# An encoder layer on one core: projection steps, scan pieces and denominators change places in the mixers

## The chip, the cores and the metric

The kernel runs on one core of a Trainium2 chip. The metric is the device time of one execution in microseconds (us). TensorE (PE in the profile; PEld is its weight load) multiplies matrices into PSUM, VectorE (DVE), ScalarE (ACT) and GpSimd (POOL) work element by element, and SyncE (SP) issues most of the transfers between memories (DMAs). Each engine works off its own instructions in order and waits for others by semaphores. The shape is fixed: 1024 tokens of width 1024, float32.

## The reference

The layer projects its input, runs two kinds of heads side by side ("mixers"), projects back, and then runs a gated feed-forward part:

```python
u      = x @ w_in                      # rq, rk, rv, rg (4 x 512), aq (512), ak, av (2 x 128)
y_ret  = silu(rg) * GroupNorm(retention_forward + retention_backward)   # 8 heads of 64
y_att  = windowed_gqa(aq, ak, av, sink)                                 # 8 heads, 2 kv heads, window 128
h      = LN1(2**0.25 * x + concat(y_ret, y_att) @ w_out)
f      = (silu(h @ w_gate) * (h @ w_up)) @ w_down + sigmoid(h @ w_pg) * (p @ w_pe)
out    = LN2(2**0.25 * h + f)
```

Retention in one direction works in chunks. Within a chunk it is `(q k^T * decay) v`. Across chunks a state is carried: each chunk makes the product `k^T v`, a scan turns these into states (state * chunk decay + product), and `q * decay` times the state is added. The backward direction does the same from the end. Attention sees, for a block of 128 queries, the blocks before, at and behind it; its scores get a bias by distance, an exponential, and a division by the sum of the exponentials plus that of a sink.

## The kernel before

Every large product is made of three matmuls on numbers split in a high and a low part (`mm3`, L83 to L86), each with 128 x 512 outputs. The whole runs in three parts: first projections, the mixers (until about 378 us), and the rest, which starts with the product by `w_out` (lines L884 to L886).

**Steps of projection as filler.** The remaining input projections stand in a list, `queue` (L286). One entry is one *step*: three matmuls of `mm3` for one block of 128 of the inner dimension. Eight steps fill half a tile and end in an eviction. `take(k)` (L291) issues the next k steps and counts them in `ticks`. Work with a due count (`later`, `side`) is issued as soon as the count of steps reaches it: so a lag is a number of steps. `run(list, total)` (L788) walks a list by hand: each `F` (None) stands for an equal share of `total` steps, everything else is called where it stands. The order of TensorE's instructions is this order exactly (`manual_schedule`, L801). VectorE, ScalarE, GpSimd and SyncE are ordered by a planner, which goes by the order of issue and by when it expects operands; an instruction wrapped in `behind` (L88) is not placed ahead of the last `mm3` issued before it.

**Mixers.** `i = 0` runs attention pair 0 first (L811 to L814), then retention pair 0 (L824). For `i = 1, 2, 3` retention pair i and attention pair i run together in one list with 48 steps (L852); they are called mixers 1, 2 and 3 below. The steps there are projections for pair i + 1, in mixer 3 the gates: gate(0) in steps 1 to 16, each half evicted by L783 to L785 after its eighth step. The last list (L866) has 16 steps.

The parts of a mixer, in the list's names:
- `K(q)`: transposes half of the retention keys; ScalarE evicts them with the decay (L428).
- `C(d)`: products k^T v of direction d (L443), into both banks "t" (forward) or both banks "s" (backward); evicted by VectorE and ScalarE (L450, L452) into `U`, whose buffer is tagged "qq" (forward) or "pt" (backward).
- `S_(d, part)`: the scan of direction d on VectorE in two pieces (L460): part 0 is one wide addition and three small ones, part 1 three small ones, one wide one, and two transfers of the result into `states` (L471).
- `sco(n)`: scores of attention block n (L583, L584), each into a bank "s"; VectorE adds the bias (L585), ScalarE takes the exponential (L588). After blocks 3 and 7 the denominators' reciprocals are made on small tiles (`sums`, L593 to L597).
- `trn(n)`: transposes block n's exponentials (L623) into banks "t"; ScalarE copies them back (L628). At n = 3 and 7 one more transposition takes the reciprocals of four blocks along (L626); they go out to memory and come back as one row for all partitions (`spread`, L601; store L608, fetch L612).
- `val(n)`: values of attention block n (L640), into a bank "o"; after n = 3 and 7 VectorE multiplies by the reciprocals (`times`, L645), LAGV steps later.
- `r.scores`: retention scores (L482) into both banks "s", then VectorE multiplies them by the decay into a tile tagged "pt" (L485).
- `Q(hh)`: VectorE multiplies queries by the decay (L496).
- `r.out`: retention output into both banks "o" (L508, L513); `E(t)` evicts it (L522 to L525).
- `M(t)`: sums of squares by a matmul (L532, L534); then, LAGS steps later each, `spread` to 128 partitions (L539), power on GpSimd (L542), store (L545), fetch as factors (L549), and on VectorE the multiplication `scaled` (L553).

There are two banks of each tag in PSUM, so a matmul that wants a bank "s" waits until the one before last is emptied. In parallel, weights of later products are split and stored to memory in the gaps (`put`, L662 to L665). `first_loads` (L859) loads the first four operands of the product by `w_out`, two into buffers tagged "w", two into buffers tagged "raw"; buffers "raw" are also used by the last split of weights, whose two halves are due at steps 50 and 53 counted from the start of mixer 3.

Of the kernel before, what the change touches and what calls it, by code (L numbers as in the profile page):

```python
# [16 lines left out]
P = 128  # L17
# [5 lines left out]
NPAIR = 4  # L23
# [7 lines left out]
LAGA = (2, 1, 4)  # L31
LAGS = (3, 6, 9, 12, 15)
LAGX = 4
LAGV = 5
NLAG = 7


# [12 lines left out]
def layer(tc, xT, xn, w_first, w_mt, w_rv, w_out, w_pg, w_pe, pT, w_gu, w_dn,  # L50
          consts, dec_b, dec_c, sink, gng, lnp, out):
    nc = tc.nc
    act, dve, pool, pe, sp = nc.scalar, nc.vector, nc.gpsimd, nc.tensor, nc.sync
# [16 lines left out]
    def bank(tag, shape=(P, HF)):  # L70
        tag = ROLE[tag]
        return ps.tile(list(shape), F32, tag=tag, bufs=NB[tag], name=nm("b" + tag))
# [21 lines left out]
    last = {}  # L94
# [62 lines left out]
    with tc.manual_schedule(engines={mybir.EngineType.DVE, mybir.EngineType.SP}):  # L157
        for kt in range(KT):
            r = xraw[kt]
# [44 lines left out]
    ident = cst[:, C_ID:C_ID + P]  # L204
# [67 lines left out]
    for h in range(2):  # L272
        sl = slice(h * HF, (h + 1) * HF)
        b = st[1, h]
        for g in range(2):
            a = slice(64 * g, 64 * g + 64)
# [129 lines left out]
    class Retention:  # L406
# [121 lines left out]
        def norm(self, t):  # L528

            b = self.o[t].rearrange("p n c -> p (n c)")  # L530
            for k in range(2):
                pe.matmul(b[0:NONE], ones, self.sq[t][k], start=k == 0, stop=k == 1)  # L532
            row = bt([2, HF], ("rb", "kv1")[t])
            behind(dve.tensor_scalar(row, b[0:2], 1.0 / 64, EPS, ALU.mult, ALU.add))  # L534
            sm, r, home = bt([P, 2, 8], "sn", 1), bt([P, HF], ("rb", "kv1")[t]), rnd[2 * self.i + t]

            def spread():
                for h in range(2):
                    sp.dma_start(sm[64 * h:64 * h + 64, 0], row[h:h + 1].rearrange("o (q e) -> o q e", e=8))  # L539

            def power():
                behind(pool.tensor_tensor(sm[:, 1], sm[:, 0], cst[:, C_MH:C_MH + 1].to_broadcast([P, 8]), ALU.pow))  # L542

            def store():
                sp.dma_start(home, sm[:, 1])  # L545

            def fetch():
                for h in range(2):
                    sp.dma_start(r[64 * h:64 * h + 64], home[64 * h:64 * h + 64].rearrange("q e -> (q e)").partition_broadcast(64))  # L549

            def scaled():
                y = self.half(t)
                behind(dve.scalar_tensor_tensor(y, y, gn[:, self.i:self.i + 1], r.rearrange("p (n c) -> p n c", c=CH),  # L553
                                                ALU.mult, ALU.mult))

            late = 0 if self.i else LAGX
            later.extend((ticks[0] + at, f) for at, f in zip(LAGS, (spread, power, store, fetch)))
            later.append((ticks[0] + LAGS[4] + late, scaled))

# [3 lines left out]
    class Attention:  # L563
# [53 lines left out]
        def turn(self, n):  # L617
            lo, hi = span(n)
            self.pt[n] = []
            for g in range(2):  # L620
                tb = bank("t", (P, 4, P))
                for kb in range(hi - lo):
                    pe.transpose(tb[:, kb, :], self.sc[n][g][:, kb * P:(kb + 1) * P], ident)  # L623
                last = not g and n % 4 == 3
                if last:
                    pe.transpose(tb[0:8, 3, :], self.st[n // 4][:, 3].rearrange("p j g -> p (j g)"), ident)  # L626
                p_ = self.sc[n][g].rearrange("p (k q) -> p k q", q=P)
                act.activation(p_[:, :hi - lo, :], tb[:, :hi - lo, :], AF.Copy)  # L628
                self.pt[n].append(p_)
                if last:  # L630
                    self.spread(n // 4, tb[0:8, 3, :])

        def values(self, n):
            hh, j = divmod(n, 4)
# [7 lines left out]
            if j == 3:  # L642
# [3 lines left out]

                later.append((ticks[0] + LAGV, times))

# [139 lines left out]
    def run(steps, total):  # L788

        shares = steps.count(None)  # L790
        done = n = 0
        for f in steps:
            if f is None:
                n += 1
                take(total * n // shares - done)
                done = total * n // shares
            else:
                f[0](*f[1:])

    F = None  # L800
    with tc.manual_schedule(engines={mybir.EngineType.PE}):  # L801
        enqueue([mtile(0, ev_av), proj_rv(), *project(1), *project(2), *project(3), gate(0), gate(1), gate(2), gate(3)])

        spare.append(bt([P, S], "aq", 3, F32R))
        twin = lambda t: t.rearrange("p (a b) -> p a b", a=2)
        ops = [twin(spare[1]), a_tile([P, 2, HF], "pro", "A0", F32R)]
        side.extend(presplit_out(0, ops, 17.5, 4))
        side.extend(presplit_out(1, ops, 44, 4, spare[:1]))
        a = Attention(0, ytile(1))
        sco, trn, val = (lambda n: (a.scores, n)), (lambda n: (a.turn, n)), (lambda n: (a.values, n))  # L810
        run([F, F, sco(0), F, sco(1), F], 16)  # L811
        run([F, (av_turn, 0), (av_turn, 1), F, trn(0), sco(2), F, trn(1), sco(3), F, trn(2), F,
             trn(3), F, val(0), val(1), val(2), val(3), sco(4), F, sco(5), F, trn(4), sco(6), F, trn(5), sco(7), F, trn(6), (decay_q, 0),
             F, trn(7), (decay_k, 0, 0), F, val(4), val(5), val(6), val(7), (decay_k, 0, 1), F], 64)  # L814
        assert not side
        y0 = ytile(0)
        side.extend(presplit_gate())
        states = state_tile()
        r = Retention(0, y0, states)
        K, M = (lambda q: (r.keys, q)), (lambda q: (r.norm, q))  # L820
        Q = lambda q: (r.queries, q)
        C, E = (lambda d: (r.kv, d)), (lambda t: (r.evict, t))
        S_ = lambda d, part: (r.scan, d, part)
        run([K(0), F, K(1), F, F, C(0), C(1), F, S_(0, 0), S_(0, 1), F, S_(1, 0), S_(1, 1), F, F, F, Q(0), F, (r.scores,), Q(1), F, F,  # L824
             (r.out,), E(0), E(1), F, (decay_q, 1), F, M(0), (decay_k, 1, 0), F, (decay_k, 1, 1), M(1)], 48)
        V = []
        for i in range(1, NPAIR):
            assert i == 1 or not side, len(side)
            r = Retention(i, ytile(2 * i), states)
            a = Attention(i, ytile(2 * i + 1))  # L830
            if i == 2:
                late = [ytile(6), ytile(7)]
                ops = [twin(late[1].bitcast(F32R)), twin(bt([P, S], "aq", 3, F32R))]
                side.extend(presplit_out(2, ops, 2, (10, 13, 16, 19, 22, 25, 28), late[:1]))
                side.extend(presplit_small(0, ops[::-1], 28.5, 34, 37.4) + presplit_small(1, ops[::-1], 39.5, 44.5, 47.9))
            elif i == 3:
                op = twin(bt([P, S], "aq", 3, F32R))
                rkx = bt([P, S], "rk", 2)
                more = []

                def spare_op(k):
                    if not more:
                        more.append(twin(bt([P, S], "rk", 2, F32R)))
                    return more[0] if k % 2 else op

                side.extend(presplit_out(3, [op, op, op, op, lambda: spare_op(1), op, lambda: spare_op(1)], 3,
                                         (8, 13.5, 19, 24.5, 30, 33.5, 37), [rkx]))
                side.extend(presplit_small(2, [op, lambda: spare_op(1)], 40, 43.5, 46.5, rkx))
                side.extend(presplit_small(3, [op, lambda: spare_op(1)], 46, 50, 53))
            G = [(f, i + 1, *x) for f, x in ((decay_q, ()), (decay_k, (0,)), (decay_k, (1,)))] if i + 1 < NPAIR else \  # L850
                [(lambda: None,)] * 3
            run([K(0), F, K(1), F, *([] if V else [F]), *V, C(0), C(1), sco(0), F, sco(1), S_(0, 0), F, trn(0), sco(2), S_(0, 1), F,  # L852
                 trn(1), sco(3), S_(1, 0), F, trn(2), S_(1, 1), F, trn(3), Q(0), F, val(0), val(1), val(2), val(3),
                 (r.scores,), sco(4), Q(1), F, sco(5), F, trn(4), sco(6), F, trn(5), sco(7), F, (r.out,), E(0), E(1), F, G[0], F,
                 M(0), G[1], F, trn(6), G[2], F, trn(7), M(1), F], 48)
            V = [val(4), val(5), val(6), val(7)]
        first_ops = []

        def first_loads():  # L859
            for kt in range(4):  # L860
                t = wp.tile([P, 2, HF], F32R, tag="w", bufs=4, name=nm("w")) if kt < 2 else \
                    wp.tile([P, 2, HF], F32R, tag="raw", bufs=2, name=nm("raw"))
                sp.dma_start(t.bitcast(F32), wod[0, kt])
                first_ops.append(t)

        run([*V, F, (first_loads,), F, F, F], 16)  # L866
        assert not side and not later

    bp.close()
# [409 lines left out]
    Q = HF // 2  # L1279
# [319 lines left out]
    n = 0  # L1599
# [343 lines left out]
    with tc.manual_schedule(engines={ET.PE, ET.DVE, ET.Activation, ET.Pool, ET.SP}):  # L1943
# [15 lines left out]
        for k in range(NG):  # L1959
# [14 lines left out]
            j = k + 1 - NG  # L1974
# [105 lines left out]
```

## Time and profile before

| | |
|---|---|
| median of 3 runs | 1181.74 us (1179.38 to 1182.0) |
| profiled execution | 1181.43 us |
| its span, first to last instruction | 1179.7 us |
| mean granted TensorE clock | 0.993 |

By stage, in that execution (starts read off TensorE's first instruction of each):

| stage | us | TensorE busy, us | granted clock | VectorE busy, us |
|---|---|---|---|---|
| until mixer 1 | 0 to 163.0 | 161.63 | 1.00 | 100.04 |
| mixer 1 | 163.0 to 225.8 | 56.78 | 0.97 | 47.44 |
| mixer 2 | 225.8 to 288.6 | 59.22 | 0.97 | 41.99 |
| mixer 3 | 288.6 to 352.9 | 59.21 | 0.97 | 43.04 |
| last steps, start of `w_out` | 352.9 to 378.4 | 25.00 | 1.00 | 15.50 |
| the rest | 378.4 to 1179.7 | 793.12 | 1.00 | 648.07 |

A row of the trace names the line, the engine, the operation and the tiles (written <- read), with the number of instructions; "idle before it" is time in which its engine did nothing, and behind the arrow stands who ended that. Busy time of TensorE says nothing about its clock: a stretch at half clock is busy too, and does half the work.

### The profile page before, as it was taken

Reading aid. Unit: us, or ns where it says so; the run is one execution under the profiler, and the core shown is the slowest. Engines: PE = TensorE matmul, PEld = TensorE weight load, DVE = VectorE, ACT = ScalarE, POOL = GpSimd, SP = SyncE. Lnnn points to the kernel's source line nnn. Section 1 sums busy time; section 2 is a strip of 40 time slices with the busy share of each in tenths; the row PEclk is TensorE's granted clock in tenths of the full one; section 3 lists DMA queues with packets and bytes.
Section 4 is the critical chain, followed back from the end, with each engine's and each line's share of the span. In section 5 each row is a group of like instructions: output and inputs, shape, how many; then the busy total and the mean of one; then the engine's idle time right before and its main releaser. Section 6 shows DMA issues by size and latency. Waiting matters only on the chain.

```text
span 1179.7 us, 19068 instructions
## 1 busy us (share of the span) xinstructions
PE 1155.0 (98%) x6978; PEld 970.6 (82%) x6978; DVE 896.1 (76%) x1687; ACT 563.7 (48%) x1162; POOL 103.5 (9%) x118
## 2 busy tenths in 40 slices
PE   9999998999899999999999999999999999999997
PEld 7888877878687888888888888888888888888885
DVE  4657668675766988957998988888888876774777
ACT  5645465757463357213454434443344445552462
POOL 2000010101000022000000000000000011134242
PEclk9999999999999999999999999999999999999999
DMA  7356776666438764766322322323223189999978
GB/s 248 95 173 218 250 234 225 211 192 200 148 135 289 283 258 170 259 214 215 116 90 99 130 103 72 134 101 115 105 83 134 72 239 336 349 245 217 261 167 229
DMA packets 88863, 218.64 MB, mean 185 GB/s; under 512 B 12544, under 2 KB 20928, under 8 KB 88768
## 3 DMA queue, kind: packets, MB, share of 16 engines
q1 hardware_dynamic: 79984, 200.11, 49.2%
q0 software_dynamic: 8784, 17.31, 8.4%
q8 instruction: 55, 0.90, 0.3%
q14 instruction: 40, 0.33, 0.1%
HBM read 143.35 MB, written 62.19 MB: 174 GB/s over the span
## 4 chain that ended last, share of the span: by engine, by line
PE 67%; DMA 2%; DVE 1%; SPq 0%; issue 0%; ACT 0%; POOL 0%; DVEq 0%; POOLq 0%
PE bmm L884 8%; PE bmm L885 8%; PE bmm L886 8%; PE bt L884 6%; PE bt L885 6%; PE bt L886 6%; PE bs L886 4%; PE bs L885 4%; PE bs L884 4%; PE bo L886 4%; PE bo L885 4%; PE bo L884 4%; DMA rnd<-sn 1%; DMA sn<-rb 0%; DVE acc L1759 0%
## 5 line engine op out<-in xcount | busy, mean ns | idle before, releaser
L84 PE MATMUL bmm<-H,w 128*128 128x512 f32 x240 | 98.5, 410 | 0.1
L85 PE MATMUL bmm<-H,w 128*128 128x512 f32 x240 | 95.7, 399 | 0.0
L86 PE MATMUL bmm<-H,w 128*128 128x512 f32 x240 | 95.0, 396 | 0.0
L1484 ACT ACTIVATE ev<-ev 128x512 f32<-128x512 f32 x42 | 26.4, 630 | 105.4 <-DVE ev L1513 92.1
L1658 POOL DMA_DIRECT2D h0b<-in_w_dn x24 | 21.6, 900 | 536.8 <-DVE ev L1464 503.6
L588 ACT ACTIVATE sc<-sc,st 128x384 f32<-128x384 f32 (+1 forms) x64 | 37.2, 583 | 39.1 <-DVE st L585 38.9
L86 PEld LDWEIGHTS bmm<-H,w 128*128 128x128 f32 x240 | 46.2, 192 | 10.6
L84 PEld LDWEIGHTS bmm<-H,w 128*128 128x128 f32 x240 | 46.1, 192 | 10.6 <-ACT H L78 0.9
L85 PEld LDWEIGHTS bmm<-H,w 128*128 128x128 f32 x240 | 46.3, 193 | 8.1
L585 DVE CUSTOM_DVE_ANT_0 sc<-cst,bs,nskb 128x384 f32<-128x384 f32 (+1 forms) x64 | 35.0, 576 | 13.5 <-PE bs L584 13.1
L1513 DVE TENSOR_TENSOR ev<-ev,bt 128x512 f32<-128x512 f32 x44 | 30.0, 682 | 12.5 <-PE bt L886 12.5
L1464 DVE TENSOR_TENSOR ev<-ev,bs 128x256 f32<-128x256 f32 x63 | 25.5, 417 | 15.6 <-PE bs L886 14.7
L1486 DVE TENSOR_TENSOR ev<-ev 128x512 f32<-128x512 f32 x42 | 29.0, 691 | 10.5 <-ACT ev L1484 9.0
L884 PE MATMUL bmm<-H,u 128*128 128x512 f32 x92 | 36.1, 392 | 0.0
L885 PE MATMUL bmm<-H,u 128*128 128x512 f32 x92 | 36.0, 392 | 0.0
L886 PE MATMUL bmm<-H,u 128*128 128x512 f32 x92 | 35.8, 389 | 0.0
L628 ACT ACTIVATE sc<-bt 128x384 f32<-128x384 f32 (+1 forms) x64 | 27.2, 455 | 15.7 <-PE bt L623 10.5
L583 PE MATMUL bs<-k,aq 128*128 128x384 f32 (+1 forms) x64 | 23.3, 369 | 11.3 <-DVE pt L485 9.2
L79 DVE TENSOR_TENSOR w<-raw,w 128x512 fp32r<-128x512 f32 x34 | 23.5, 695 | 13.6 <-ACT w L78 13.0
L884 PE MATMUL bmm<-H,w 128*128 128x512 f32 x84 | 32.9, 392 | 0.0
L885 PE MATMUL bmm<-H,w 128*128 128x512 f32 x84 | 32.9, 392 | 0.0
L886 PE MATMUL bmm<-H,w 128*128 128x512 f32 x84 | 32.7, 389 | 0.0
(832 smaller groups left out, 3842.6 us busy)
## 6 DMA issues: line engine op xcount, KB each, us to landing
ad<-ev SPq DMA_DIRECT2D x33, 512.0 KB
pgd<-pro SPq DMA_DIRECT2D x28, 512.0 KB, 3.3
raw<-in_w_gu SPq DMA_DIRECT2D x22, 512.0 KB
ln<-in_w_gu SPq DMA_DIRECT2D x22, 512.0 KB
raw<-ad SPq DMA_DIRECT2D x40, 256.0 KB, 6.0
ln<-ad SPq DMA_DIRECT2D x37, 256.0 KB, 6.1
H<-in_w_dn SPq DMA_DIRECT2D x33, 256.0 KB, 9.3
wod<-aq SPq DMA_DIRECT2D x16, 512.0 KB, 2.6
```

Of the source, the lines that this page charges most:

```text
L84: pe.matmul(o, lh, rh, start=start, stop=False)
L85: pe.matmul(o, lh, rl, start=False, stop=False)
L86: recent[0] = pe.matmul(o, ll, rh, start=False, stop=stop).ins.name
L585: dve.tensor_tensor_reduce(sc[g][:, :nk], cst[:, tc0:tc0 + nk], b[:, :nk], slope(i, g), nskb[:, 2 * i + g:2 * i + g + 1], ALU.add, ALU.min ...
L588: act.activation(sc[g][:, :nk], sc[g][:, :nk], AF.Exp, bias=st_[:, 0, j, g:g + 1], scale=-1.0, accum_out=st_[:, 2, j, g:g + 1])
L628: act.activation(p_[:, :hi - lo, :], tb[:, :hi - lo, :], AF.Copy)
L884: pe.matmul(o, lh, rh, start=start, stop=False, skip_group_check=True)
L885: pe.matmul(o, lh, rl, start=False, stop=False, skip_group_check=True)
L886: pe.matmul(o, ll, rh, start=False, stop=stop, skip_group_check=True)
L1484: act.activation(c[:, 0, :], c[:, 0, :], AF.Silu)
L1486: dve.tensor_tensor(c[:, 1, :], c[:, 0, :], c[:, 1, :], ALU.mult)
L1513: dve.tensor_tensor(get(name), ev[left][:, m, :], right, ALU.add)
```

## The change

```diff
-LAGV = 5
+LAGV = 7
...
-            late = 0 if self.i else LAGX
+            late = LAGX if self.i + 1 < NPAIR else 0
...
-                last = not g and n % 4 == 3
+                last = not g and n == 7
...
+        def sums_turn(self):
+            tb = bank("t", (P, 4, P))
+            pe.transpose(tb[0:8, 3, :], self.st[0][:, 3].rearrange("p j g -> p (j g)"), ident)
+            self.spread(0, tb[0:8, 3, :])
...
-             trn(3), F, val(0), val(1), val(2), val(3), sco(4), F, ...
+             trn(3), F, val(0), val(1), val(2), val(3), (a.sums_turn,), sco(4), F, ...
...
-            run([K(0), F, K(1), F, *([] if V else [F]), *V, C(0), C(1), sco(0), F, sco(1), S_(0, 0), F, trn(0), sco(2), S_(0, 1), F,
-                 trn(1), sco(3), S_(1, 0), F, trn(2), S_(1, 1), F, trn(3), Q(0), F, val(0), val(1), val(2), val(3),
-                 (r.scores,), sco(4), Q(1), F, sco(5), F, trn(4), sco(6), F, trn(5), sco(7), F, (r.out,), E(0), E(1), F, G[0], F,
+            run([K(0), F, K(1), F, *([] if V else [F]), *V, C(0), C(1), F, sco(0), S_(0, 0), F, sco(1), S_(0, 1), F, trn(0), sco(2), S_(1, 0), F,
+                 trn(1), sco(3), S_(1, 1), F, trn(2), F, trn(3), Q(0), F, (a.sums_turn,), val(0), val(1), val(2), val(3),
+                 (r.scores,), Q(1), F, sco(4), F, sco(5), F, trn(4), sco(6), F, trn(5), sco(7), F, (r.out,), E(0), E(1), F, G[0], F,
                  M(0), G[1], F, trn(6), G[2], F, trn(7), M(1), F], 48)
...
-        run([*V, F, (first_loads,), F, F, F], 16)
+        run([(first_loads,), *V, F, F, F, F], 16)
```

- The mixers' lists get two more shares F: one between `C(1)` and `sco(0)`, one between `r.scores` and `sco(4)`. The steps stay 48, so each share is smaller.
- The scan's four pieces stand one place earlier in the list: `S_(0, 0)` behind `sco(0)` and no longer behind `sco(1)`, and so on.
- The first half's reciprocals are transposed by themselves in `sums_turn`, with a bank of their own: in mixers 1 to 3 one share behind turn 3 and ahead of the values; in the attention of i = 0 behind the values. The second half's stay in turn 7.
- `times` is due 7 and not 5 steps behind the values.
- `scaled` is due 4 steps later in mixers 1 and 2, as it was for i = 0 already; in mixer 3 it isn't.
- In the last list the four first loads stand ahead of the last values and the first four steps.

The step count at which each part of a mixer stands (48 n / shares, cut down), before and after:

| part | mixer 1 | mixers 2, 3 |
|---|---|---|
| C(0), C(1) | 8 -> 7 | 5 -> 5 |
| sco(0) | 8 -> 9 | 5 -> 7 |
| S_(0, 0) | 10 -> 9 | 8 -> 7 |
| S_(0, 1) | 13 -> 12 | 11 -> 10 |
| trn(0), sco(2) | 13 -> 14 | 11 -> 12 |
| S_(1, 0) | 16 -> 14 | 14 -> 12 |
| trn(1), sco(3) | 16 -> 16 | 14 -> 15 |
| S_(1, 1) | 18 -> 16 | 16 -> 15 |
| trn(2) | 18 -> 19 | 16 -> 17 |
| trn(3) | 21 -> 21 | 19 -> 20 |
| first denominators | 21 -> 24 | 19 -> 22 |
| val, r.scores | 24 -> 24 | 22 -> 22 |
| sco(4) | 24 -> 26 | 22 -> 25 |
| sco(5) | 26 -> 28 | 25 -> 27 |
| trn(4), sco(6) | 29 -> 31 | 28 -> 30 |
| r.out, E | 34 -> 36 | 33 -> 35 |
| M(0) | 40 -> 40 | 39 -> 40 |
| M(1) | 45 -> 45 | 45 -> 45 |

More of the change, by code (lines that the diff above doesn't have):

```diff
@@ L812, in layer @@
         run([F, (av_turn, 0), (av_turn, 1), F, trn(0), sco(2), F, trn(1), sco(3), F, trn(2), F,
-             trn(3), F, val(0), val(1), val(2), val(3), sco(4), F, sco(5), F, trn(4), sco(6), F, trn(5), sco(7), F, trn(6), (decay_q, 0),
+             trn(3), F, val(0), val(1), val(2), val(3), (a.sums_turn,), sco(4), F, sco(5), F, trn(4), sco(6), F, trn(5), sco(7), F, trn(6), (decay_q, 0),
              F, trn(7), (decay_k, 0, 0), F, val(4), val(5), val(6), val(7), (decay_k, 0, 1), F], 64)
```

## The prediction

> **What bounds the kernel now.** I read the page first, then who waited for whom, then TensorE in order of time, then the queues behind the waits found. The first two lines of the page, and TensorE's rows in the view of waits (engine and line, whom for: us in total, times, longest):
>
> ```profile
> span 1179.7 us, 19068 instructions
> ## 1 busy us (share of the span) xinstructions
> PE 1155.0 (98%) x6978; PEld 970.6 (82%) x6978; DVE 896.1 (76%) x1687; ACT 563.7 (48%) x1162; POOL 103.5 (9%) x118
> ```
>
> ```profile
> PE bs L583 <- DVE pt L485: 9.2, 3, 3.4
> PE bt L626 <- DVE st L597: 2.4, 2, 1.4
> PE bs L583 <- ACT pt L452: 2.2, 3, 0.7
> ...
> PE bt L443 <- ACT pt L428: 0.5, 1, 0.5
> PE bt L623 <- ACT sc L628: 0.4, 1, 0.4
> PE bt L884 <- ACT h0b L1064: 0.3, 1, 0.3
> ```
>
> TensorE sets the time: what it computes isn't changed, so a change of order can win only its idle time and what follows from that. Three rows have three, two and three cases: they are one pattern, repeated in mixers 1 to 3. TensorE in order of time (start, us, line, tiles, idle before it and its releaser), two of the three waits in full and two matmuls a step apart:
>
> ```profile
> 188.40 0.28 PE L626 MATMUL bt<-cst,st 128*8 128x128 f32 x1 [1.38 <-DVE st L597]
> ...
> 189.54 0.40 PE L84 MATMUL bmm<-H,w 128*128 128x512 f32 x1
> ...
> 190.23 0.40 PE L84 MATMUL bmm<-H,w 128*128 128x512 f32 x1
> ...
> 198.17 0.58 PE L583 MATMUL bs<-k,aq 128*128 128x384 f32 x1 [3.44 <-DVE pt L485]
> ```
>
> ```profile
> 259.50 0.49 PE L583 MATMUL bs<-k,aq 128*128 128x384 f32 x1 [2.42 <-DVE pt L485]
> ```
>
> ```profile
> 323.64 0.44 PE L583 MATMUL bs<-k,aq 128*128 128x384 f32 x1 [3.34 <-DVE pt L485]
> ```
>
> The three long waits are all `sco(4)`, which follows `r.scores` with nothing between: it needs a bank of PSUM that only the multiplication L485 empties. One projection step is 0.69 us (189.54 to 190.23). The stretches view just behind each long wait (stretch, its length, then busy us of PE, PEld, DVE, ACT, POOL; granted clock, DMA share, GB/s) shows what it costs besides:
>
> ```profile
> 198.33:201.73 3.40, 3.40 (x10) 2.71 (x11) 2.23 (x6) 1.96 (x5) 0.00 (x0) 0.50 0.40 117
> ...
> 259.77:263.17 3.40, 3.40 (x10) 2.62 (x10) 1.52 (x5) 1.41 (x4) 0.00 (x0) 0.50 0.70 189
> ...
> 324.62:328.02 3.40, 3.40 (x10) 2.72 (x9) 1.52 (x5) 1.88 (x5) 0.00 (x0) 0.50 0.26 78
> ```
>
> The clock is at half for 3.40 us each time: half of it, 1.7 us, is lost, 5.1 us in all, and TensorE counts as busy meanwhile. The Trainium skill ("TensorE: Matmul & The Clock Gate", section "Why this matters for your kernels") asks only that no idle gap exceed about 3 us; by that rule the 2.42 us of mixer 2 should have cost no clock, and the term would be 3.4 us and not 5.1. The trace disagrees: 2.42 us was enough here.
>
> What L485 itself waits for, mixer by mixer: VectorE's rows of the scan's last addition (L460) and of L485, and SyncE's row of the transfer between them (L471):
>
> ```profile
> 191.28 0.67 DVE L460 SCALAR_TENSOR_TENSOR pt<-pt,cd 128x448 f32<-128x448 f32 x1
> ...
> 197.43 1.29 DVE L485 TENSOR_TENSOR pt<-bs,dt 128x512 f32<-128x512 f32 x2 [1.27 <-DMA states<-pt]
> ```
>
> ```profile
> 192.09 1.21 SPq L471 DMA_DIRECT2D states<-pt  x2
> ```
>
> ```profile
> 253.00 0.68 DVE L460 SCALAR_TENSOR_TENSOR pt<-pt,cd 128x448 f32<-128x448 f32 x1
> ...
> 258.76 1.29 DVE L485 TENSOR_TENSOR pt<-bs,dt 128x512 f32<-128x512 f32 x2 [1.89 <-DMA states<-pt]
> ```
>
> ```profile
> 253.74 1.34 SPq L471 DMA_DIRECT2D states<-pt  x2
> ```
>
> ```profile
> 316.21 0.68 DVE L460 SCALAR_TENSOR_TENSOR pt<-pt,cd 128x448 f32<-128x448 f32 x1
> ...
> 322.90 1.29 DVE L485 TENSOR_TENSOR pt<-bs,dt 128x512 f32<-128x512 f32 x2 [4.80 <-DMA states<-pt]
> ```
>
> ```profile
> 316.92 1.17 SPq L471 DMA_DIRECT2D states<-pt  x2
> ```
>
> The scores are written into the buffer `pt` that still holds the backward scan's states, so the path is scan, transfer, multiplication, `sco(4)`. From the end of the addition to L485 it is 5.5, 5.1 and 6.0 us; SyncE issues the transfer within 0.2 us of the addition's end each time.
>
> **The change part by part**, by the table of steps in the section on the change.
>
> *`sco(0)` behind two steps.* It waits 0.7 us three times for the eviction of the state products. Two steps are 1.4 us, so the wait goes: **-2.1** (-2.2 to 0).
>
> *First denominators in a turn of their own.* Waits of 1.38 us in mixer 1 and, from the 2.4 us of both, 1.0 in mixer 3, at the end of turn 3. The transposition now comes two steps (mixers 2, 3) or three (mixer 1) later, 1.4 to 2.1 us, which covers both: **-2.4**, worst case 0. No instruction is added. The copy behind it, the store and the fetch move along; their reader L645 is put two steps later (LAGV), and still has five or six steps until `r.out` wants its bank.
>
> *`sco(4)` behind `queries(1)` and a share of steps.* Its due time on TensorE moves by +2, +3, +3 steps: +1.4, +2.1, +2.1 us. The waits gone ahead of it pull it forward by 0.7 to 2.1 us in each mixer, so that alone nothing much would be won; the transfer has to land earlier too.
>
> *The scan a place up.* Its last piece is issued one or two steps and turn 2 earlier, the piece before it two steps and turn 1. But the scan isn't held by its place. Turn 2 of mixer 3, behind which its last piece is issued now:
>
> ```profile
> 309.70 0.82 PE L623 MATMUL bt<-cst,sc 128*128 128x128 f32 x6
> ```
>
> The scan ends at 316.9, some 7 us behind that, as VectorE works off a queue. What leaves that queue ahead of it:
>
> ```profile
> 237.88 0.75 DVE L553 SCALAR_TENSOR_TENSOR y<-y,gn,rb 128x512 f32<-128x512 f32 x1 [0.96 <-DMA rb<-rnd]
> ```
>
> ```profile
> 311.23 0.68 DVE L784 SCALAR_TENSOR_TENSOR sq<-sq,bmm 128x512 f32<-128x512 f32 x1
> ...
> 312.03 0.68 DVE L785 SCALAR_TENSOR_TENSOR y<-sq,y 128x512 f32<-128x512 f32 x1
> ```
>
> In mixer 3 the gate's eviction of step 16 (L784, L785: 1.36 us) falls behind the last piece, now at step 15, and so does the second L553 (0.75, step 16 with the later factors). In mixer 2 the first L553 also stops holding VectorE for 0.96. With the first addition no longer behind `sco(1)`, I estimate the scan's end 3 us earlier; nothing (0) and 4 us are the bounds. At the transfer times above, L485 then comes 3 us earlier against due times that move by -0.7 (mixer 1: +1.4 - 0.7 - 1.4), +1.4 (2) and +0.4 us (3). The waits become 3.44 - 3 + 0.7 = 1.1, 2.42 - 3 - 1.4 = none, 3.34 - 3 - 0.4 = none. The sum: **-8.1** of 9.2.
>
> *The clock.* A wait of 1.38 us (188.40) was followed by full clock. With 1.1 us at most left, all three slow stretches go: **-5.1**.
>
> *What it costs.* In mixer 1 five steps instead of six stand between the keys' transposition and C(0), which already waits 0.5 for its operands: **+0.7**. The 48 steps are cut into 19 or 20 turns instead of 17 or 18, and VectorE is late all through the first half: attention turns follow their scores by five steps where it was six. Nearest row: turn 3's 0.4 us wait for ScalarE, L628. I take 0.3 a mixer, **+1.0** (0 to 3.0).
>
> *First attention (i = 0) and LAGV there.* TensorE shows no wait in it; nothing.
>
> *Loads ahead of the last values.* This touches the end of the mixers, where TensorE just waits for retention's last factors. VectorE's and SyncE's rows, then pieces of the chain that ended last:
>
> ```profile
> 351.04 0.68 DVE L534 TENSOR_SCALAR kv<-bo 2x512 f32<-2x512 f32 x1 [2.88 <-PE bo L532]
> ...
> 359.07 0.69 DVE L664 TENSOR_TENSOR rk<-raw,rk 128x512 fp32r<-128x512 f32 x1 [0.70 <-ACT rk L663]
> ```
>
> ```profile
> 355.21 1.96 SPq L539 DMA_DIRECT2D sn<-kv  x2
> ...
> 361.20 0.93 SPq L863 DMA_DIRECT2D raw<-wod  x2
> ```
>
> ```profile
> 353.80 1.40 DMA rnd<-sn
> ...
> 363.73 6.61 DMA rnd<-sn
> ...
> 378.48 0.50 PE bt L884
> ```
>
> The sums of M(1) leave TensorE at 351; their spread is issued at 355.2, the factors are stored at 363.7, and that small store takes 6.61 us behind loads issued at 361.2, where the one before took 1.40. With the loads issued four steps (2.8 us) earlier, the last store should be free of them, and the earlier ones hit. What can be won is the 0.3 us that TensorE waits; I take **0** (-0.6 to +7.1, below).
>
> Sum: -2.1 - 2.4 - 8.1 - 5.1 + 0.7 + 1.0 = **-16.0 us**. The profiled execution took 1181.43 (span 1179.7), the median is 1181.74: so 1165.4 against the one and **1165.7** against the other. All behind the mixers is busy without a wait and only moves forward.
>
> **The rivals.**
>
> *The transfer lands no earlier* (the queue on VectorE, not the place, sets the scan). Then `sco(4)` starts when it does now, earlier waits won are lost there again, and the gain is the steps put ahead of it: 1.4 + 2.1 + 2.1 = 5.6 us. The wait of mixer 2 shrinks to about 1 us, which saves one slow stretch, 1.7: 1181.7 - 7.3 = **1174.4**. For it: 7 us behind its place. Against it: the work that leaves the queue.
>
> *SyncE is held by a load at the end.* If a load into `raw` stands before M(0)'s store, SyncE is held until that buffer is split (359.07 + 0.69 = 359.8), and M(1)'s spread leaves 5.4 us late (two issues behind it, 360.6 for 355.2). If the last store still collides, TensorE idles those 5.4 us and loses 1.7 of clock: 1165.7 + 7.1 = **1172.8**. For it: the load is now asked for ahead of the split that frees its buffer by five steps, not one. Against it: the order is planned by expected readiness.
>
> *Slower: SyncE is held before the transfer of states.* It issues in order, and once waited long for two stores of split weights:
>
> ```profile
> 302.34 7.60 SPq L665 DMA_DIRECT2D wod<-aq  x2
> ```
>
> If such a wait comes to stand between an earlier scan's end (3 us) and its transfer, that leaves 7.6 - 3 = 4.6 us later than now in each mixer: 3 x 4.6 - 5.6 = +8.2, **1190**. It decides from 1.9 us of delay a mixer (5.6 / 3). For it: puts keep their steps while the scan moves past them. Against it: in none of the three mixers did the transfer wait for SyncE now.
>
> *No change:* the first two rivals together, -7.3 + 7.1: **1181.5**.
>
> **How the numbers follow.** Forecast 0.58, first rival (wholly or halfway, 1168 to 1175) 0.20, end of the mixers 0.12, slower 0.06, none 0.04. Faster 0.90, same 0.04, slower 0.06, with 0.2% (2.4 us) as what a measurement can tell from no change. All gone with nothing given back and the 0.3 won: 2.2 + 2.4 + 9.2 + 5.1 + 0.3 = 19.2, 1162.5. Low **1162**, high **1175** takes in the first two rivals.
>
> **What would show it.** The row of L583 behind L485 falls from 9.2 to about 1 us, that behind L452 and that of L626 vanish; no stretch at half clock between 150 and 380 us; L460's last addition nearer to C(1) by 3 us; in 378 to the end the same durations. Wrong would be: waits over 2 us still at `sco(4)` (first rival), an idle TensorE ahead of L884 (second), SyncE's L665 long before L471 (third).

## The result, and the profile after

The changed kernel takes 1167.95 us in the median of four runs (1165.79 to 1169.73); the kernel before, measured beside it, 1181.45. The ratio is 0.9888, with a 95% interval of 0.9867 to 0.9909: 13.5 us faster. A second measurement (a0 below) gave 1166.88 against 1183.08 (0.9868, 0.9844 to 0.9891): 16.2 us faster. The profiled execution is the fastest of the four, 1165.79 us; against the profiled one before, its span is 15.7 us shorter.

The first lines of the page of the changed kernel, and its TensorE rows in the view of waits:

```profile
span 1164.0 us, 19072 instructions
## 1 busy us (share of the span) xinstructions
PE 1149.6 (99%) x6978; PEld 967.1 (83%) x6978; DVE 896.2 (77%) x1687; ACT 563.4 (48%) x1162; POOL 103.8 (9%) x118
```

```profile
PE bt L623 <- ACT sc L628: 2.6, 3, 1.8
...
PE bt L443 <- ACT pt L428: 1.0, 1, 1.0
PE bt L635 <- DVE st L597: 0.8, 1, 0.8
PE bs L583 <- DVE st L585: 0.6, 1, 0.6
```

The rows of L583 behind L485 (9.2) and behind L452 (2.2) are gone, and so is that of L626 (2.4). L623 behind ScalarE has grown (0.4 before). New are L635, the transposition in `sums_turn`, and L583 behind the bias of the block before (L585). (Lines behind L633 stand five higher in the changed kernel.) The stretches view over all the mixers gives the sum. First the kernel before, then the changed one (columns as in the prediction):

```profile
150.00:380.00 230.00, 214.74 (x2176) 178.54 (x2175) 158.05 (x337) 136.83 (x335) 18.75 (x20) 0.98 0.61 200
```

```profile
150.00:380.00 230.00, 225.04 (x2244) 187.78 (x2243) 172.00 (x359) 146.67 (x354) 19.44 (x20) 1.00 0.66 216
```

TensorE idles 230 - 225.04 = 5.0 us where it idled 15.3, so 10.3 us are idle time saved. The granted clock is 1.00, and no stretch at half clock is left, which is worth 5.1 us more. Together that is 15.4 of the 15.7 us.

The chain behind `sco(4)` in mixer 3. The keys' products C(1) start it; before, they ended at 296.52 + 1.04 = 297.56:

```profile
296.52 1.04 PE L443 MATMUL bs<-rv,pt 64*64 64x64 f32 x58
```

In the changed kernel, TensorE, VectorE and SyncE in order of time:

```profile
287.10 1.04 PE L443 MATMUL bs<-rv,pt 64*64 64x64 f32 x58
...
312.80 0.34 PE L583 MATMUL bs<-k,aq 128*128 128x384 f32 x1
```

```profile
304.53 0.68 DVE L460 SCALAR_TENSOR_TENSOR pt<-pt,cd 128x448 f32<-128x448 f32 x1
...
310.71 1.29 DVE L485 TENSOR_TENSOR pt<-bs,dt 128x512 f32<-128x512 f32 x2 [1.75 <-PE bs L482]
```

```profile
305.24 1.10 SPq L471 DMA_DIRECT2D states<-pt  x2
```

The scan ends 305.21 - 288.14 = 17.1 us behind C(1), where it was 19.3. L485 waits for TensorE's scores and no longer for the transfer: that has landed earlier. And `sco(4)` at 312.80 has no wait. One reason that the transfer lands earlier is the scan. The other is the transfer itself. The view of DMA issues (KB each, median us from issue to landing), before and after:

```profile
states<-pt SPq DMA_DIRECT2D x2, 240.0 KB, 5.2
```

```profile
states<-pt SPq DMA_DIRECT2D x2, 240.0 KB, 3.0
```

Before, a load of 512 KB into `raw` and a store of 512 KB into `wod` were issued 2.2 and 1.4 us ahead of the transfer (SyncE's rows of the kernel before):

```profile
314.73 0.34 SPq L118 DMA_DIRECT2D raw<-in_w_mt  x1
315.53 0.33 SPq L665 DMA_DIRECT2D wod<-aq  x1
```

In the changed kernel the transfer passed both. In mixer 1 it takes 3.0 us where it took 4.6; for mixer 2 the view shows no landing.

The cost of the change sits mostly in mixer 1. TensorE's rows of turns 2 and 3, then ScalarE's:

```profile
186.20 0.93 PE L623 MATMUL bt<-cst,sc 128*128 128x128 f32 x6 [1.76 <-ACT sc L628]
...
189.04 0.93 PE L623 MATMUL bt<-cst,sc 128*128 128x128 f32 x6 [0.54 <-ACT sc L628]
```

```profile
183.46 0.63 ACT L668 ACTIVATE pro<-pre 128x512 fp32r<-128x512 f32 x1 [4.02 <-DMA pgd<-pro]
...
185.67 0.85 ACT L628 ACTIVATE sc<-bt 128x384 f32<-128x384 f32 x2
```

The split of weights in `put` (L668) writes a buffer whose last store (`pgd<-pro`) is still under way. ScalarE works in order, so it stands still for 4.02 us. The exponentials of blocks 2 and 3 and the copies of turn 1 (L628), which empty the banks that turn 2 needs, are queued behind it. In the kernel before, the same put stood behind these copies and was held for 1.26 us:

```profile
181.74 0.87 ACT L628 ACTIVATE sc<-bt 128x384 f32<-128x384 f32 x2
183.87 0.63 ACT L663 ACTIVATE pro<-pre 128x512 fp32r<-128x512 f32 x1 [1.26 <-DMA pgd<-pro]
```

### The profile page after: what moved, and what is told of

It is laid out like the page before. It is cut to its first block, busy times and chain, and to the rows that moved or that the text cites. A ratio compares the mean times of both kernels' runs of the same rounds, so it can differ in the third digit from the quotient of the medians.

```text
span 1164.0 us, 19072 instructions
## 1 busy us (share of the span) xinstructions
PE 1149.6 (99%) x6978; PEld 967.1 (83%) x6978; DVE 896.2 (77%) x1687; ACT 563.4 (48%) x1162; POOL 103.8 (9%) x118
## 4 chain that ended last, share of the span: by engine, by line
PE 93%; DVE 3%; DMA 2%; ACT 1%; issue 1%; SPq 0%; DVEq 0%; ACTq 0%
PE bmm L889 8%; PE bmm L890 8%; PE bmm L891 8%; PE bt L889 6%; PE bt L890 6%; PE bt L891 6%; PE bmm L84 5%; PE bmm L85 5%; PE bmm L86 5%; PE bs L891 4%; PE bs L890 4%; PE bs L889 4%; PE bo L891 4%; PE bo L890 4%; PE bo L889 4%; PE bo L645 2%
## 5 line engine op out<-in xcount | busy, mean ns | idle before, releaser
L84 PEld LDWEIGHTS bmm<-H,w 128*128 128x128 f32 x240 | 45.2, 188 | 10.8 <-ACT H L78 1.1
L86 PEld LDWEIGHTS bmm<-H,w 128*128 128x128 f32 x240 | 45.2, 188 | 10.1
L85 PEld LDWEIGHTS bmm<-H,w 128*128 128x128 f32 x240 | 45.3, 189 | 7.6
L588 ACT ACTIVATE sc<-sc,st 128x384 f32<-128x384 f32 (+1 forms) x64 | 37.2, 582 | 15.7 <-DVE st L585 15.6
L585 DVE CUSTOM_DVE_ANT_0 sc<-cst,bs,nskb 128x384 f32<-128x384 f32 (+1 forms) x64 | 35.0, 576 | 7.5 <-PE bs L584 7.5
L889 PE MATMUL bmm<-H,u 128*128 128x512 f32 x92 | 36.1, 392 | 0.0
L628 ACT ACTIVATE sc<-bt 128x384 f32<-128x384 f32 (+1 forms) x64 | 27.0, 457 | 16.3 <-PE bt L623 13.7
L889 PE MATMUL bmm<-H,w 128*128 128x512 f32 x84 | 33.0, 392 | 0.0
L1469 DVE TENSOR_TENSOR ev<-ev,bo 128x256 f32<-128x256 f32 x70 | 28.3, 417 | 5.1 <-PE bo L891 4.4
```

Source lines behind the costliest of these rows:

```text
L84: pe.matmul(o, lh, rh, start=start, stop=False)
L85: pe.matmul(o, lh, rl, start=False, stop=False)
L86: recent[0] = pe.matmul(o, ll, rh, start=False, stop=stop).ins.name
L585: dve.tensor_tensor_reduce(sc[g][:, :nk], cst[:, tc0:tc0 + nk], b[:, :nk], slope(i, g), nskb[:, 2 * i + g:2 * i + g + 1], ALU.add, ALU.min ...
L588: act.activation(sc[g][:, :nk], sc[g][:, :nk], AF.Exp, bias=st_[:, 0, j, g:g + 1], scale=-1.0, accum_out=st_[:, 2, j, g:g + 1])
L889: pe.matmul(o, lh, rh, start=start, stop=False, skip_group_check=True)
```

## The experiments

The theory: each of three parts was needed for `sco(4)` (the scan's place, the later factors, the share ahead of it), and the separate denominators for the rest; what the change gave back is ScalarE's hold by the put. The rivals: the place doesn't matter because VectorE's queue sets the scan; one part does all; the loads at the end bring the gain. Every ratio is to the kernel before, measured beside it on the same chip: 1183.18 us for the first four, 1183.08 for the next four, 1182.87 for the last two. The changed kernel has two measurements, the one above and a0, on the chip of the second group. Of the first four runs only e1 is clear of both by time. The interval of e3 overlaps with one of them, those of e2 and e4 with both, so for these three the argument rests on the waits in the traces.

### e1: the scan back at its places

```diff
-C(0), C(1), F, sco(0), S_(0, 0), F, sco(1), S_(0, 1), F, trn(0), sco(2), S_(1, 0), F,
-trn(1), sco(3), S_(1, 1), F, trn(2), F, trn(3), Q(0), F, (a.sums_turn,), ...
+C(0), C(1), F, sco(0), F, sco(1), S_(0, 0), F, trn(0), sco(2), S_(0, 1), F,
+trn(1), sco(3), S_(1, 0), F, trn(2), S_(1, 1), F, trn(3), Q(0), F, (a.sums_turn,), ...
```

> The changed kernel with the scan's four pieces back one place in the mixers' lists. Theory A (place and queue both set the scan): its last addition ends 2 to 3 us later behind C(1) (17.8, 15.7 and 17.1 us in the changed kernel, 19.6, 18.9 and 19.3 before), and since sco(4) has 0.4 to 1.5 us to spare, waits of 0.5 to 2 us at L583 behind L485 come back in two or three mixers: 1169.5 to 1173 us. Theory B (the steps ahead of sco(4) do it alone): no such wait, 1168 within 1 us. Theory C (VectorE's queue sets the scan, place does nothing): the scan ends where it does in the changed kernel, 1168.

1175.86 us, 0.9941 (0.9929 to 0.9954). By the ratios of the changed kernel, 0.9888 and 0.9868, the place is worth 6 to 9 us in the new list. It isn't the state of the kernel before: with the share ahead of `sco(0)`, the pieces come up to two steps later than there, and in mixers 1 and 3 the scan ends later behind C(1). The view of waits of this run:

```profile
PE bs L583 <- DVE pt L485: 7.1, 3, 3.1
```

The three waits are 3.12, 1.56 and 2.38 us. The scan ends 22.5, 18.3 and 20.5 us behind C(1), against 17.8, 15.7 and 17.1 in the changed kernel (and 19.6, 18.9 and 19.3 in the kernel before): place does move it, by 2.6 to 4.7 us, more than expected. So the rival that VectorE's queue alone sets the scan falls. The transfers of the states take 4.0 to 4.7 us from issue to landing, against 3.0 in mixers 1 and 3 of the changed kernel, with other transfers issued within 1.5 us ahead of them. In mixers 2 and 3 L485 waits for them (0.68 and 0.96 us). In mixer 1 it doesn't: it starts when VectorE's queue gets to it, 5.6 us behind the scan. The stretches behind the first and the third wait:

```profile
200.50:203.80 3.30, 3.30 (x9) 2.67 (x9) 1.34 (x5) 1.42 (x4) 0.00 (x0) 0.50 0.97 307
...
321.50:324.90 3.40, 3.40 (x15) 2.55 (x16) 3.21 (x8) 1.11 (x3) 0.00 (x0) 1.00 0.53 181
```

3.12 us of idling brought half clock; 2.38 us did not.

### e2: no share ahead of `sco(4)`

```diff
-(r.scores,), Q(1), F, sco(4), F, sco(5), F,
+(r.scores,), sco(4), Q(1), F, sco(5), F,
```

> The changed kernel with no share of steps between r.scores and sco(4). Theory A: L485 can't start until the scores are done and takes 0.7 us for the bank that sco(4) wants, so 0.8 to 1.2 us of waiting come back in each mixer, too short for the half clock: 1170 to 1171.5 us. Theory B (the steps do it alone): the waits come back at 1.5 to 3 us with slow stretches behind them, 1174 to 1178. Theory D (the scan's place alone does it): 1168 within 1 us.

1171.4 us, 0.9901 (0.9887 to 0.9914). The view of waits:

```profile
PE bs L583 <- DVE pt L485: 4.7, 3, 2.8
```

0.94 and 0.94 us in mixers 1 and 2, and 2.82 in mixer 3. Mixer 3's transfer went out 1.5 us behind a load into `raw` here, and a stretch at half clock follows the wait. With the scan moved, the share takes off the last 0.9 us, and more only where the transfer meets a large one.

### e3: the first denominators back in turn 3

```diff
-                last = not g and n == 7
+                last = not g and n % 4 == 3
...
-trn(2), F, trn(3), Q(0), F, (a.sums_turn,), val(0), ...
+trn(2), F, trn(3), Q(0), F, val(0), ...
```

The attention of i = 0 is put back in the same way.

> The changed kernel with the first denominators back in turn 3, in the first attention too. Theory A: in mixer 3 the reciprocals are ready at 306.6 and turn 3 ends its six transpositions at 304.3, so 2.3 us of waiting where 0.8 is now, and 0.6 in mixer 1: 1169.5 to 1171 us. Rival: with the scan out of VectorE's way the reciprocals come early enough and the turn is worth nothing, 1168 within 1 us.

1172.13 us, 0.9909 (0.9896 to 0.9923). The view of waits:

```profile
PE bt L626 <- DVE st L597: 3.8, 2, 2.5
PE bt L623 <- ACT sc L628: 3.0, 2, 2.7
```

The wait comes back in mixer 2 (1.29) and mixer 3 (2.48, with half clock behind it), while in mixer 1 ScalarE's hold takes its place (2.69, with half clock too). By the two ratios of the changed kernel the turn of its own is worth 2.5 to 4.9 us in the new order, as much as forecast or more, since one of the waits left without it is long enough for half clock. Not all of that need be the turn's: this execution also waits 1.1 us ahead of the product by `w_out` (L889).

### e4: the factors early again

```diff
-            late = LAGX if self.i + 1 < NPAIR else 0
+            late = 0 if self.i else LAGX
```

> The changed kernel with the multiplication by retention's factors 4 steps earlier again in mixers 1 and 2 (so at steps 7 and 12 of mixers 2 and 3). Theory A: VectorE is held for up to 1 us by the factors' transfer and the second multiplication stands inside the scan again; the scan ends 1 to 1.5 us later in mixers 2 and 3, which the spare time of sco(4) takes up: 1168 to 1169.5 us. Rival (the factors are what lets the scan end earlier): 2 us or more later, waits at L583 behind L485 come back, 1171 or more.

1171.2 us, 0.9901 (0.9886 to 0.9916). The view of waits, and VectorE's row of the factors in mixer 2:

```profile
PE bs L583 <- DVE st L585: 2.8, 4, 1.1
...
PE bs L583 <- DVE pt L485: 0.6, 1, 0.6
```

```profile
234.31 0.75 DVE L553 SCALAR_TENSOR_TENSOR y<-y,gn,rb 128x512 f32<-128x512 f32 x1 [2.73 <-DMA rb<-rnd]
```

VectorE stands still for 2.73 us on factors that haven't come back from memory. The scan of mixer 2 ends 18.7 us behind C(1), 3.0 later, yet the share ahead of `sco(4)` covers that; the 0.6 us are mixer 3's. The most is paid at other scores, whose banks VectorE empties late with the bias (L585). So the part does save waits (2.8 us here, 0.6 in the changed kernel), by a way that neither theory had named; for `sco(4)` it matters little.

### a0: the changed kernel again

> The changed kernel itself, unchanged, on the chip of the next three, as their measure. Ratio to before 0.987 to 0.990 as first measured. Its runs should differ by about 1.7 us in two groups, with granted clocks of 0.999 and 0.996, if the wait of 1.76 us ahead of turn 2 in mixer 1 sometimes grows long enough for a stretch at half clock.

1166.88 us; the ratio stands at the top. ScalarE's row:

```profile
184.08 0.63 ACT L668 ACTIVATE pro<-pre 128x512 fp32r<-128x512 f32 x1 [5.09 <-DMA pgd<-pro]
```

Held for 5.09 instead of 4.02 us, it makes TensorE wait 2.83 us at turn 2 instead of 1.76, and now half clock follows (the stretches view):

```profile
186.20:189.50 3.30, 2.68 (x10) 2.39 (x11) 2.62 (x9) 3.30 (x12) 0.00 (x0) 0.50 0.84 213
```

One and the same kernel thus has the slow stretch in one execution and not in another, as the store lands. The two groups of runs that were expected aren't told apart by the clock: it is 0.998 in the runs of 1165.48 and 1166.3, and 0.997 in those of 1167.46 and 1168.36.

### e5: the first loads back

```diff
-        run([(first_loads,), *V, F, F, F, F], 16)
+        run([*V, F, (first_loads,), F, F, F], 16)
```

> The changed kernel with the four first loads back behind the first four steps of the last list. Theory A: the last store of factors again stands behind three of the loads, and TensorE waits 0.3 to 1.5 us for the product by w_out's last operand: 0.3 to 1.5 us slower than the changed kernel. Rival (the end of the mixers has room now): no wait ahead of L889, the same time within 0.5 us.

1167.07 us, 0.9871 (0.9852 to 0.9889), 0.2 us from a0. The rival is right: these loads bring nothing that can be measured.

### e6: no share ahead of `sco(0)`

```diff
-C(0), C(1), F, sco(0), S_(0, 0), F, sco(1), ...
+C(0), C(1), sco(0), S_(0, 0), F, sco(1), ...
```

> The changed kernel without the share of steps between C(1) and sco(0), so that 48 steps are cut into 18 or 19 shares. Theory A: the wait of sco(0) for the eviction of the state products comes back, 0.7 us in each mixer, 2.1 in all, nothing else: 2 us slower than the changed kernel. Rival (the share only moves a wait from here to a later place, as shares get smaller): the waits at turns 1 to 3 shrink by as much, same time within 0.7 us.

1167.79 us, 0.988 (0.986 to 0.9901), 0.9 us above a0, which these runs don't resolve. The view of waits:

```profile
PE bs L583 <- DVE pt L450: 3.2, 3, 1.1
PE bs L583 <- ACT pt L452: 2.1, 3, 0.7
PE bt L623 <- ACT sc L628: 1.4, 1, 1.4
```

5.3 us are back at `sco(0)`, yet the wait at turn 2 is gone with its half clock, and so are the 0.8 and 0.6 us of mixer 3. The 1.4 us stand at turn 3 of mixer 1. TensorE's row of that turn, and ScalarE's of the put:

```profile
188.47 0.92 PE L623 MATMUL bt<-cst,sc 128*128 128x128 f32 x6 [1.37 <-ACT sc L628]
```

```profile
186.51 0.63 ACT L668 ACTIVATE pro<-pre 128x512 fp32r<-128x512 f32 x1 [1.40 <-DMA pgd<-pro]
```

In this order the put comes behind the copies of turn 1 again, which start at 182.05 us, and is held for 1.40 us only. So e6 takes away more than the share: it also moves the put in ScalarE's queue, and doesn't price the share by itself. Between 150 and 380 us TensorE idles 230 - 222.27 = 7.7 us here at full clock. That is 2.7 us more than in the first profiled execution of the changed kernel, and about as much as the 6.0 us of a0 with the 1.7 us of its slow stretch.

### e8: the put later, the denominators behind the values

```diff
-        at = [2 + 2.8 * k for k in range(14)] + [58.5 + 2.5 * k for k in range(7)] + ...
+        at = [2 + 2.8 * k for k in range(14)] + [58.5, 61, 66.5, 68.5, 70.7, 72.9, 75] + ...
...
-F, (a.sums_turn,), val(0), val(1), val(2), val(3),
+F, val(0), val(1), val(2), val(3), (a.sums_turn,),
```

The third put in mixer 1 comes three steps later, behind turn 2's copies.

> The changed kernel with two more moves: in mixer 1 the third weight put of the gate's third block 3 steps later (63.5 to 66.5, the four behind it 2.5 to 0.5 steps later), and in all mixers the first denominators' turn behind the four values. Theory A (ScalarE, held 4.0 us by that put until an earlier store lands, is what makes turn 2 of mixer 1 wait): its waits of 1.76 and 0.54 us go, and so does the wait of 0.8 us in mixer 3: 3 us less wait, and no run with a second slow stretch: 3 to 4 us faster than the changed kernel. Rival (ScalarE is simply full there): the waits stay within 0.5 us, and only the 0.8 goes.

1164.45 us, 0.9847 (0.9825 to 0.9869), 2.4 us below a0 on the same chip; the runs of the two just overlap (1162.35 to 1165.96, and 1165.48 to 1168.36). The view of waits:

```profile
PE bmm L84 <- issue: 1.6, 1, 1.6
...
PE bt L889 <- ACT h0b L1069: 1.0, 1, 1.0
...
PE bt L623 <- ACT sc L628: 0.3, 1, 0.3
```

ScalarE's hold and TensorE's wait at turn 2 are gone, and that is the put's doing, since the other edit stands behind turn 3. The 0.54 us at turn 3 of mixer 1, also ahead of the other edit, are gone with it, and so are the 0.8 us of L635 in mixer 3. It gains less than the 3 to 4 us expected, because 1.0 us of waiting appears at the product by `w_out` and 1.6 us at one place behind `r.out`, for which the trace shows no releaser. The causes of both stay open.

### e9: a large transfer put ahead of the states

```diff
-(8, 13.5, 19, 24.5, 30, 33.5, 37), [rkx]))
+(12, 16.5, 19, 24.5, 30, 33.5, 37), [rkx]))
```

Two steps of the split in mixer 3 are due later, and the planned order of the loads follows.

> The changed kernel with two stores of split weights in mixer 3 due 3.5 and 2.5 steps later (8 to 11.5 or 12, 13.5 to 16), so that SyncE's planned order has one of them and the load of the next weights right ahead of the transfer of the backward states; mixers 1 and 2 are as in the changed kernel. Theory F (the transfer takes 3.0 us when no 512 KB transfer was issued in the 2.7 us before it, and 4.3 to 7 us behind one): in mixer 3 it takes 4.5 us or more where it took 3.0, L485 waits for it and not for the scores, and sco(4) waits up to 1.5 us; in mixers 1 and 2 nothing changes; 1167 to 1170 us. Rival (its time depends on how many bytes the queues hold in all, or varies by chance): 3.0 to 3.4 us as in the other mixers, no wait.

SyncE, VectorE and the view of DMA issues in mixer 3 of this run:

```profile
305.39 0.34 SPq L118 DMA_DIRECT2D raw<-in_w_mt  x1
305.99 1.10 SPq L471 DMA_DIRECT2D states<-pt  x2
```

```profile
312.40 1.29 DVE L485 TENSOR_TENSOR pt<-bs,dt 128x512 f32<-128x512 f32 x2 [3.28 <-DMA states<-pt]
```

```profile
states<-pt SPq DMA_DIRECT2D x2, 240.0 KB, 5.2
```

A load of 512 KB 0.6 us ahead makes the transfer 5.2 us long instead of 3.0. Mixer 1's transfer in the same run, with nothing so close ahead, took 3.0. So in mixer 3 the shorter transfer after the change comes from what is issued ahead of it, and not from the chip or the run. The time is 1167.08 us, 0.9867 (0.985 to 0.9883), no worse than the changed kernel, and `sco(4)` has no wait, where up to 1.5 us were expected: the share and the earlier scan had left 1.4 us to spare. The shorter transfer is thus not needed for the gain in mixer 3. This execution also waits 1.2 us ahead of the product by `w_out`; the cause is open.

### e10: the best version

e8 with a second buffer for the sums of squares, and in mixer 1 the second keys' transposition a share earlier.

```diff
-bt([P, 2, 8], "sn", 1)
+bt([P, 2, 8], "sn", 2)
...
-run([K(0), F, K(1), F, *([] if V else [F]), *V, C(0), ...
+run([K(0), *([F] if V else []), K(1), F, *([] if V else [F, F]), *V, C(0), ...
```

> The kernel of e8 with two buffers of 64 bytes instead of one for the spread sums (tag sn), and in mixer 1 the second half of the keys transposed without steps ahead of it, so three shares stand between it and C(0). Theory A: the wait of 1.2 us ahead of C(0) in mixer 1 goes; in the last mixer the spread of M(1) no longer waits for the store of M(0), which brings the last factors 2 to 3 us earlier, so that the wait of 0.95 us ahead of the product by w_out goes: 2 us faster than e8, 0.983 of the kernel before. Rival (SyncE's order, not the buffer, holds the spread; and ScalarE, not the place, the keys): no change from e8 within 0.7 us.

1163.26 us, 0.9838 (0.9824 to 0.9853). All its runs (1162.57 to 1165.35) are faster than all of e9 on the same chip (1166.68 to 1169.41) and of the changed kernel in both measurements. The view of waits:

```profile
PE bt L623 <- ACT sc L628: 1.3, 3, 0.6
PE bt L443 <- ACT pt L428: 1.3, 1, 1.3
```

The wait at `w_out` is gone in this trace. C(0) still waits for ScalarE's last eviction, which ends at 170.1 us where it ended at 170.2 in the changed kernel: the keys' earlier place doesn't move it. The gain over e8, about 1 us, is within the spread.

Not tried: a buffer of its own for the retention scores, which would take the transfer off the path.

## Why the prediction was right, and where it was off

The forecast was 1165.7, and the median is 1167.95, 2.2 us above it. The forecast change was -16.0 us; the two measurements gave -13.5 and -16.2. Point by point:

- **What bounds the kernel** was right: 15.4 of 15.7 us are TensorE's idle time and its half clock in the mixers.
- **`sco(0)`**, -2.1: gone (2.2). What it is worth by itself stays open: without the share the median is 0.9 us higher, which isn't resolved, and e6 moves the put as well.
- **First denominators**, -2.4: 2.4 became 0.8, so -1.6. In mixer 3 the reciprocals (L597) end 18.5 us behind C(1), where it was 16.3: 2.1 us later, and the move was not enough.
- **`sco(4)`**, -8.1: all 9.2 us. The scan ended 1.8, 3.2 and 2.2 us earlier behind C(1), not 3; the step that kept "the transfer times above" was wrong in the other direction, as the transfer went from 4.6 to 3.0 us in mixer 1 and from 5.2 to 3.0 us in mixer 3. Queue and place both count for the scan's end: e4 shows 3.0 us in mixer 2 from the factors, e1 2.6 to 4.7 from the place. But what the prediction lets leave VectorE's queue in mixer 3 didn't leave it (rows below the list), so the estimate of 3 us came near for another reason than its own.
  In mixer 1 the sum would have left 3.44 - 1.8 + 0.7 = 2.3 us of waiting, and none was left. There `sco(4)` comes 197.20 - 172.24 = 25.0 us behind C(1), where it would have come at 22.4 without its wait before. The sum had it 0.7 us earlier; it comes 2.6 us later, and the waits of 2.3 us at turns 2 and 3 and C(1) a step earlier make up most of the difference. Where the waits are gone (e8), the scan of mixer 1 ends 14.4 us behind C(1), and `sco(4)` still has no wait.
- **The clock**, -5.1: right for the three waits. A 1.76 us wait was followed by full clock, as the prediction's 1.38. The Trainium skill ("TensorE: Matmul & The Clock Gate", section "Why this matters for your kernels") puts the limit at gaps of about 3 us; here 2.42 us (before), 2.43 (e9), 2.48 (e3), 2.55 (e5), 2.69 (e3), 2.82 (e2) and 2.83 us (a0) were each followed by half clock, 2.38 us (e1) once was not. The measurement decides: about 2.4 us can already be too long. Only one wait on either side lies that close, so a sharp limit isn't shown.
- **C(0)**, +0.7: 0.5 became 1.0. TensorE comes to C(0) 0.65 us earlier (168.91 us, before 169.56), and ScalarE's last eviction of the keys ends where it did (170.3 us before, 170.2 after). What sets that end is ScalarE's queue and not the steps between the keys and C(0): e10 gives the keys more steps, and the wait stays.
- **Attention turns**, +1.0 at 0.3 a mixer: this is the term that failed. L623's row went from 0.4 to 2.6, and scores behind L585 took 0.6 more: 2.8 us in the profiled execution, inside the 0 to 3.0 of the term, with 2.3 us of waits in mixer 1. The nearest row (0.4) didn't show what was to come, because its mechanism was another: the order on ScalarE changed, a put whose step had stayed came to stand ahead of the copies of turn 1, and it waits there for a store (4.02 us, where it was 1.26 behind them). The slower rival had this sentence, "puts keep their steps while the scan moves past them", but for SyncE alone. Where the hold is longer, as in a0, the half clock comes on top, 1.7 us. This is part of what lies between the fastest run and the median: the mean granted clock is 0.999 in the runs of 1165.79 and 1167.54, and 0.996 in those of 1168.36 and 1169.73. Of these four only the fastest was traced, so for the others the slow stretch is inferred from the clock; it was seen in a0 and, with mixer 1's order unchanged, in e5 and e9. The run of 1167.54 is 1.75 us above the fastest at the same clock, and that is not explained.
- **The loads**, 0: right (e5).

By rows, -2.2 - 1.6 - 9.2 - 5.1 + 0.5 + 2.2 + 0.6 - 0.3 (L884's row) = -15.1 against -15.7 of the spans.

VectorE's queue in mixer 3 of the changed kernel, ahead of the scan's last addition at 304.53 us:

```profile
301.46 0.75 DVE L553 SCALAR_TENSOR_TENSOR y<-y,gn,kv 128x512 f32<-128x512 f32 x1
...
302.33 0.69 DVE L789 SCALAR_TENSOR_TENSOR sq<-sq,bmm 128x512 f32<-128x512 f32 x1
...
303.13 0.69 DVE L790 SCALAR_TENSOR_TENSOR y<-sq,y 128x512 f32<-128x512 f32 x1
```

The second L553 and the gate's eviction of step 16 (L784 and L785 before, L789 and L790 now) should have fallen behind the addition, whose place in the list is a step ahead of theirs. They still run ahead of it. What left the queue are mainly the three multiplications of queries (L496) that ran between C(1) and the scan's end before, and one of three weight splits.

The rivals: the transfer did land earlier, so the first fell. That e1 comes out near its time (1175.86, forecast 1174.4) is luck: its scan ends 22.5, 18.3 and 20.5 us behind C(1), not as in the kernel before. No idle time ahead of the first product by `w_out` in the changed kernel; 1.0 to 1.2 us in e3, e8 and e9 show that it isn't far. SyncE was never held ahead of the transfer. (The 7.60 us of its L665 row, which priced this rival, are two issues with 6.9 us between them; that would make 6.1 us of the 8.2.)

## What to carry to other kernels

When steps are moved in a hand-made order, go through every in-order queue that they cross and look for an instruction that keeps its step and can wait for a transfer: here a weight split on ScalarE made TensorE wait 1.8 to 2.8 us in one place. The list's order isn't the order on the other engines: the forecast named what would fall behind the scan on VectorE, and other instructions did. A small transfer on the critical path is priced with what is issued on its queue in the two microseconds ahead of it, not by its last duration. And waits don't simply add up: taking one share out brought 5.3 us of waits back at one place and took others away, and ScalarE's order had changed with it.

## What the runs showed of the hardware

The time of one small transfer depends on its neighbours more than expected. The 240 KB of states took 3.0 us where nothing large was issued in the 3.8 us ahead (mixer 3 of the changed kernel, e3 and e8), and 3.8 to 6.1 us where 512 KB were issued 0.6 to 1.5 us ahead (e1, e2, e8, e9, e10 and the kernel before). In between it varies: with a load of 512 KB 2.2 us ahead, in mixer 1, it took 3.0 us in the changed kernel, 3.3 in a0 and 4.1 in e3. So the distance to the nearest large load isn't all. The Trainium skill ("DMA: Bandwidth & Descriptors", section "Queues, rings and completion order") says that each DMA engine consumes the descriptors of a ring in their order, which agrees with the 5.2 us of e9, where a load was moved ahead of the transfer.

And the clock falls to half after waits so near to those of this kernel that one program does or doesn't meet it, by how long one store takes to land: 1.76 us of waiting in one execution, 2.83 in another, and 1.7 us of clock between them.
